# Hybrid trunk in Strassen pairs: value sums into SBUF, conv borders kept in the tile, gate weights split at another place, and more instructions tied to written order

## The chip, the cores and the metric

The kernel runs on one core of a Trainium2 chip. Five engines of the core have queues of their own and are synchronised by semaphores: TensorE (PE in the profile; its weight loads are PEld), VectorE (DVE), ScalarE (ACT), GpSimd (POOL) and SyncE (SP), which here only issues DMAs. Each queue is worked off in its order. The metric is the device time of one execution in microseconds; lower is better. The time of a kernel is the median of several executions; beside it stands one execution taken with the profiler, from which all rows of the profile come.

## The reference

Two layers of a decoder trunk on 1024 tokens of width 1024, all in float32. A layer normalises x, projects it with one wide matrix, runs four mLSTM heads and four retention heads of width 256 in chunks, gates them and projects back.

```python
for l in range(DEPTH):                                   # DEPTH = 2
    ada = silu(c) @ w_ada[l] + b_ada[l]
    shift, scale, gate = split(ada, 3)
    h = rmsnorm(x, norm_g[l]) * (1 + scale) + shift
    p = h @ w_in[l]
    mq, mk, mv, mo, mz, mi, mf, rq, rk, rv, rz = split_cols(p)
    qk = silu(causal_dwconv(concat(mq, mk), conv_w[l], conv_b[l]))   # 4 taps along the tokens
    cell = mlstm_chunkwise(*heads(qk), heads(mv), mi + b_igate[l], mf + b_fgate[l])
    y_m = sigmoid(mo) * head_layernorm(cell, gn_m[l]) * silu(mz)
    ret = retention_chunkwise(rotary(rq), rotary(rk), rv)
    y_r = head_layernorm(ret, gn_r[l]) * silu(rz)
    x = x + gate * (concat(y_m, y_r) @ w_out[l])
return rmsnorm(x, final_g)
```

causal_dwconv is a sum of four products of a weight with the input shifted by 0 to 3 tokens.

## The kernel before, in words

**Numbers in two parts.** Every operand of a matmul is kept as a high part (a copy rounded to the fp32r format, on ACT) and a low part (the difference, on POOL or DVE); mm3 (L172 to L175) makes three matmuls of a product: high·high, high·low, low·high. For a weight these are `high` (L397, the copy at L399) and `low` (L402, the subtraction at L404). For data it is `split_to` (L853: the copy at L854, the subtraction at L855).

**Strassen pairs.** Two column blocks of the projection and the two halves of the tokens make a 2 × 2 product, computed with seven block products, a11, a12, S1, S2, S3, S4, a22. `quad` (L682) prepares the weights. A plain weight is a load from SP; S1 and S3 are a load and then a second DMA, issued from POOL, that adds another block onto it (`add`, L693); S2 and S4 are sums on DVE (`total`, L697). The `Feeder` issues these steps by slot numbers: the load eight slots ahead of use, the add six, the high copy some four, the low part two. One slot is one product of twelve matmuls or two of them. The products are added up in three PSUM banks X, Y and Z: `pair_product` (L741) for q, k, z and o, `vpair_product` (L769) for the values. In the latter, a11 is copied out of X (L802) and added to what Y holds; before, the sum stood in Y itself (L803) and `store` read it from there in two steps, the high copy on ACT (L774) and the subtraction on DVE (L779).

**The order of the work.** PE's order is written out by hand for the whole kernel. `launch` puts a generator of follow-up work on a list; `tick`, called after each product, advances those whose time has come; the number after a `yield` is how many ticks later it goes on. On the other engines Tile's scheduler decides the order by its own estimate of times, within priorities, except for instructions that are marked with `late` (L133): those stay in the order in which the program was written, behind everything written earlier on that engine. `Later()` does the same for a string of DVE instructions. The start of layer 0 (from L1416, until startup.\_\_exit\_\_) is a script of two- to four-letter steps that fixes the order on all engines: Ann a step of the conditioning's sums, Tnn transposes of x, Hnn, Enn, Unn, Cnn the modulation (L1515, L1517, L1521, L1525), Fnn and fnn the first matmuls (L1473 to L1477), Pn and Gn the sums and the resulting scales, Wnn and wnn weights.

**Gate weights.** The input and forget gates have eight columns of weights. `gate_raw` (L474) loads them into a tile wgr, of which there is one buffer; `gate_units` (L480) spreads them into a 36-column tile in two parts (L485 fills the gap with zeros, then two `split_to`) and multiplies. `gate_chain` (L495) then computes the running gate sums on DVE with a helper whose instructions show as L140, and PE transposes them (L554, the tiles T4). `rotary_tables` is another long string of small DVE instructions of layer 0.

**Convolution.** `conv_chain` (L857) scales the last tap on ACT (L861), adds three shifted taps on DVE (L867), applies tanh (L872) and multiplies (L874). The first half of the tokens leaves its last three columns in a small tile, halo (L863); in the second half the taps cover only 511, 510 and 509 columns, and three tiny instructions (L869) add what comes over the border from the halo.

**Attention.** `attention` loads chunks of q and k back from DRAM, splits them (`split_qk`, L983: ACT's L854 and POOL's L855 with q and kc), and the scores multiply q with kc. Small statistics go over DVE and POOL (L1150 to L1164).

**Plan.** A string lists the order of the pair jobs in each layer: v45 are the values of heads 4 and 5, q4 and k4 the query and key of head 4, z4 its gate path, a10 a z and an o block together.

Of the kernel before, what the change touches and what calls it, by code (L numbers as in the profile page):

```python
# [87 lines left out]
def tile_hybrid_trunk(ctx, tc, x, xt, c, positions, w_ada, b_ada, norm_g, w_in, w_blk, w_val, conv_w, conv_b,  # L88
# [23 lines left out]
    def wt(tag, n, bufs, dt=F32):  # L112
        return wrk.tile([P, n], dt, tag=tag, bufs=bufs, name=nm(tag))

# [15 lines left out]
    def f(ap):  # L130
        return ap.bitcast(F32)

    def late(ins):  # L133
        tc.keep_in_program_order(ins)
        return ins
# [343 lines left out]

    def gate_units(gr, hT, pgs):  # L480
        wg = (wt("cH", 516, 1, F32R)[:, 0:KT * 36], wt("cL", 516, 1, F32R)[:, 0:KT * 36])
        gr3 = gr.rearrange("p (k g) -> p k g", k=KT)
        w3 = [w.rearrange("p (k g) -> p k g", k=KT) for w in wg]
        for w in w3:
            A.activation(w[:, :, 4:32], ones.unsqueeze(1).to_broadcast([P, KT, 28]), AF.Copy, scale=0.0)  # L485
        for a, b in ((0, 4), (32, 0)):
            split_to((w3[0][:, :, a:a + 4], w3[1][:, :, a:a + 4]), gr3[:, :, b:b + 4], V)
        for half in range(2):
            pg = ps_a()
            for k in range(KT):  # L490
                mm3(pg[0:36, :], [w[:, k * 36:(k + 1) * 36] for w in wg], hT[k][half], k == 0, k == KT - 1)
            pgs.append(pg)
            yield

    def gate_chain(l, pgs, gt):  # L495
# [19 lines left out]
        for half in range(2):  # L515
            A.activation(es[half][0:4], es[half][0:4], AF.Ln, bias=ones[0:4, 0:1])
        yield 7
        T4s = []
# [141 lines left out]
    class Feeder:  # L660
# [21 lines left out]
        def quad(self, blk, at, u):  # L682
            raw, r, h = {}, {}, {}
            a11, a12, a21, a22 = blk[0][0], blk[0][1], blk[1][0], blk[1][1]

            def ev(t, fn, *args):
                self.events.append((t, lambda: fn(*args)))

            def load(n, src):
                raw[n] = ring_load(src)  # L690

            def add(n, src):
                G.dma_start(raw[n], src, accum_op=ALU.add)  # L693

            def total(n, one, two):
                raw[n] = raw[one]
                V.tensor_tensor(raw[n], raw[one], raw[two], ALU.add)  # L697

            def hi(n):
                h[n] = high(raw[n])  # L700

            def lo(n, eng):
                r[n] = low(h[n], raw[n], eng)

            for n, one, two in (("S1", a21, a22), ("S3", a21, a11)):
                ev(at[n] - 8, load, n, one)
                ev(at[n] - 6, add, n, two)
            for n, src in (("a11", a11), ("a12", a12), ("a22", a22)):
                ev(at[n] - 7 + u, load, n, src)
            for n in at:  # L710
                if n not in ("S2", "S4"):
                    ev(at[n] - 4 + u, hi, n)
                    ev(at[n] - 2, lo, n, G if n in POOL_LOW else V)
            T2, T4 = at["S2"], at["S4"]
            ev(T2 - 4, total, "S2", "a11", "S1")
            if at["a12"] < T2:
                ev(T2 - 3, total, "S4", "a12", "S2")
            ev(T2 - 4 + u, hi, "S2")
            ev(T2 - 2 - (T4 - T2 < 3), lo, "S2", V)
            if at["a12"] > T2:  # L720
                ev(T4 - 3, total, "S4", "S2", "a12")
            ev(T4 - 4 + u, hi, "S4")
            ev(T4 - 2, lo, "S4", V)
            return r, h
# [15 lines left out]

    def pair_product(F, done, loose=False):  # L741
        bank, keep = {}, {}

        def product(n, part, w):
            b, form = PRODUCT[n]
            new = b not in bank
            if new:
                bank[b] = ps_x() if b == "X" else ps_z()
            for k in range(4):
                mm3(bank[b], w[k], F[form][k], new and k == 0, k == 3, b != "Y")  # L750
            with tc.high_priority():
                if n in ("a11", "S1", "S2"):
                    keep[n] = wt("acc", 512, NACC)
                    A.copy(keep[n], bank[b])  # L754
                elif n == "a12":
                    c = keep["a11"] if loose else bank["Y"]
                    V.tensor_tensor(c, bank["Y"], keep["a11"], ALU.add)
                    done(0, 0, c)
                elif n == "S3":
                    V.tensor_tensor(keep["S1"], bank["X"], keep["S1"], ALU.add)  # L760
                    done(1, 1, keep["S1"])
                elif n == "S4":
                    V.tensor_tensor(keep["S2"], bank["Z"], keep["S2"], ALU.add)  # L763
                    done(0, 1, keep["S2"])
                else:
                    done(1, 0, bank["X"])
        return product

    def vpair_product(l, F, heads):  # L769
# [15 lines left out]
        def product(n, part, w):  # L785
# [13 lines left out]
            with tc.high_priority():  # L799
                if n == "a11":  # L800
                    c = wt("acc", 512, NACC)
                    A.copy(c, bank["X"])  # L802
                    V.tensor_tensor(bank["Y"], bank["Y"], c, ALU.add)  # L803
                    launch(store(part, 0, 0, bank["Y"]))
                    del bank["Y"]
                elif n in ("S1", "S2"):
# [49 lines left out]

    def conv_chain(l, hg, which, m, half, pt, halo):  # L857
        cl = cols[l][0]
        ct = which * 8 + hg * 2 + m
        acc = wt("acc", 512, NACC)  # L860
        A.activation(acc, pt, AF.Identity, bias=cl[:, 8 + ct:9 + ct], scale=cl[:, 72 + ct:73 + ct])  # L861
        if half == 0:
            V.tensor_copy(halo, pt[:, HALF - 3:HALF])  # L863
        yield 1
        for d in range(1, 4):
            wcol = cl[:, 24 + 16 * (3 - d) + ct:25 + 16 * (3 - d) + ct]
            V.scalar_tensor_tensor(acc[:, d:], pt[:, 0:HALF - d], wcol, acc[:, d:], ALU.mult, ALU.add)  # L867
            if half:
                V.scalar_tensor_tensor(acc[:, 0:d], halo[:, 3 - d:3], wcol, acc[:, 0:d], ALU.mult, ALU.add)  # L869
        yield 1  # L870
# [46 lines left out]
    def conv_done(l, hg, which):  # L917
        halos = [wt("halo", 3, 4) for _ in range(2)]
        late = []

        def one(m, half, src, delay=0):
            launch(conv_chain(l, hg, which, m, half, src, halos[m]), delay)

        def done(m, half, src):
            if m and half:
                late.append(src)
                return
            one(m, half, src)
            if m:
                one(1, 1, late[0], 1)  # L930
        return done
# [34 lines left out]
    def attention(l, hg, gt):  # L966
# [16 lines left out]
        def split_qk(what, j):  # L983
            if j < NCH:
                raw = raws.pop((what, j))
                t = wt("q", 1024, 2, F32R) if what == "q" else wt("kc", 1024, 1, F32R)
                (kx if what == "k" else qs)[j] = t
                split_to((t[:, 0:512], t[:, 512:1024]), raw)

# [367 lines left out]
    def norm_later(l, xn, sq, hT, half, keep, gaps):  # L1357
# [19 lines left out]
        for k in range(KT):  # L1377
            gain, shift = gsh[l][:, 0, k:k + 1], gsh[l][:, 1, k:k + 1]
            hT[k][half] = (bt(F32R), bt(F32R))
            V.tensor_tensor(xn[k], xn[k], R, ALU.mult)  # L1380
            A.activation(hT[k][half][0], xn[k], AF.Identity, scale=gain, bias=shift)
# [73 lines left out]
    for l in range(DEPTH):  # L1455
# [23 lines left out]
        if l == 0:  # L1479
# [10 lines left out]
            for step in script.split():  # L1490
# [46 lines left out]
                elif what == "P":  # L1537
                    ada_sums(0, arg[0], accs[arg[0]], pad)
                elif what == "G":
                    n = arg[0]  # L1540
# [9 lines left out]
            head_cols(0, hrows)  # L1550
            startup.__exit__(None, None, None)
        else:
            for half in range(2):
                for k in range(KT):
                    first(half, k)
                    tick()
                if half == 0:
                    drain()
        for half in range(2):
            z_evac(gp, 0)(half, pf[0][half])  # L1560
            o_evac(gp, 0, gdr[l][0])(half, pf[1][half])
            z_evac(gp, 1)(half, pf[2][half])
        if l == 0:
            for r in ring3:
                A.activation(r[:, :, HD:HD + 2], ident[:, 0:8].rearrange("p (a c) -> p a c", a=4), AF.Copy, scale=0.0)
                A.copy(r[:, 0:2, HD:HD + 1], rmask[:, 254:256].unsqueeze(2))
        F = {}
        launch(build_forms(hT, F))
        run_units(gate_units(gate_raw(l) if l else vgr, hT, pgs))
        launch(gate_chain(l, pgs, gt), 1)  # L1570
        if l == 0:
# [7 lines left out]
        plan = ("v45 v67 z4 q4 k4 z5 q5 k5 v01 q6 k6 q7 z6 k7 q0 a10 k0 v23 q1 k1 a11 q2 k2 q3 a20 k3 z7 a21 a30 a31",  # L1579
                "v45 q4 k4 z4 q5 k5 v67 q6 k6 z5 q7 k7 v01 q0 k0 z6 a10 q1 k1 v23 q2 k2 a11 q3 k3 a20 z7 a21 a30 a31")[l]  # L1580
        jobs = [(w[0], [int(d) for d in w[1:]]) for w in plan.split()]
# [17 lines left out]
        def job_product(what, arg):  # L1599
# [10 lines left out]
            if h > 3:  # L1610
                return pair_product(F, rot_done(l, h, which, *rot), True)
            return pair_product(F, conv_done(l, h, which))

# [86 lines left out]
```

## Time and profile before

| | us |
|---|---|
| median of three executions (lowest, highest) | 2282.63 (2281.71, 2287.09) |
| the profiled execution | 2286.23 |
| its span, first to last instruction | 2284.5 |
| mean granted clock of TensorE in it, as a share of full speed | 0.972 |

How to read the rows: L174 is line 174 of the kernel. An entry such as "PE pz L173 <- DVE acc L779: 16.0, 3, 7.6" means that PE's instructions of L173 which write a tile pz stood still for 16.0 us in all, three times, at most 7.6, until DVE's instruction of L779 had written acc. In a row of the timeline the first number is the start, the second the duration, and the bracket the idle time of that engine before it and what ended it. A row of windows gives the stretch, its length, the busy time of PE, PEld, DVE, ACT and POOL with the number of instructions, then the granted clock of TensorE, the share of the DMA engines and the rate in GB/s. A group's row gives count, then busy us in all and mean ns, then idle time of the engine before it and what ended it.

### The profile page before, as it was taken

To read this page: it belongs to the slowest core of one execution; us is meant where nothing else is said; L and a number is where in the kernel's file an instruction comes from. 1 tells how busy PE (TensorE), PEld (TensorE's weight loads), DVE (VectorE), ACT (ScalarE), POOL (GpSimd) and SP (SyncE) were. 2 spreads that over 40 slices of the span, in tenths; PEclk is the share of its full clock that TensorE was granted. 3 is DMA by queue.
4 is the path that set the end of the run, shared out by engine and by line. 5 is a ranking of instruction groups with operands and counts; after the bars stand their busy time and mean duration, and the time that the engine had idled before them with its cause. 6 is when DMAs were issued, how large, how long until landed. Compare 5 with 4: busy or idle time off the path is not lost. (4 is left out here: it accounts for less than half of the span.)

```text
span 2284.5 us, 35248 instructions
## 1 busy us (share of the span) xinstructions
PE 2134.0 (93%) x11483; PEld 1840.7 (81%) x11483; DVE 1827.6 (80%) x3301; ACT 1150.6 (50%) x2157; POOL 957.2 (42%) x842
## 2 busy tenths in 40 slices
PE   5979899999999998999999799999999899899998
PEld 3778789878897877888787788988988888688887
DVE  5898888888979999893627989698697789977653
ACT  5634344444555656653456333544555555565442
POOL 0343244444354544514266434544635353442323
PEclk8999999999999999999999899999999999999999
DMA  8247678887686767686633676877867677576974
GB/s 261 66 116 217 192 233 228 237 240 190 180 244 166 191 183 188 194 268 212 215 126 79 201 197 194 245 193 204 245 159 207 183 205 196 155 205 198 261 256 118
DMA packets 452549, 448.32 MB, mean 196 GB/s; under 512 B 191218, under 2 KB 309754, under 8 KB 452364
## 3 DMA queue, kind: packets, MB, share of 16 engines
q1 hardware_dynamic: 432636, 410.14, 58.0%
q0 software_dynamic: 19584, 35.66, 10.4%
q8 instruction: 90, 1.47, 0.3%
q14 instruction: 95, 0.78, 0.1%
q10 hardware_dynamic: 144, 0.26, 0.0%
HBM read 322.69 MB, written 123.24 MB: 195 GB/s over the span
## 5 line engine op out<-in xcount | busy, mean ns | idle before, releaser
L399 ACT CAST wH<-R 128x512 fp32r<-128x512 f32 x616 | 378.2, 618 | 463.7 <-PE px L174 122.1
L404 POOL TENSOR_TENSOR R<-R,wH 128x512 fp32r<-128x512 f32 x276 | 395.9, 1441 | 508.1 <-ACT wH L399 344.2
L173 PE MATMUL px<-b,wH 128*128 128x512 f32 x912 | 365.1, 400 | 11.1 <-ACT acc L754 8.2
L174 PE MATMUL px<-b,wH 128*128 128x512 f32 x912 | 362.7, 398 | 0.0
L175 PE MATMUL px<-b,R 128*128 128x512 f32 x912 | 361.7, 397 | 0.0
L404 DVE TENSOR_TENSOR R<-R,wH 128x512 fp32r<-128x512 f32 x340 | 258.4, 764 | 112.3 <-ACT wH L399 107.5
L174 PE MATMUL pz<-b,wH 128*128 128x512 f32 x704 | 276.2, 392 | 5.1 <-DVE b L1251 5.1
L173 PE MATMUL pz<-b,wH 128*128 128x512 f32 x704 | 276.6, 393 | 1.9 <-DVE acc L763 1.8
L175 PE MATMUL pz<-b,R 128*128 128x512 f32 x704 | 275.3, 391 | 0.0
L173 PEld LDWEIGHTS px<-b,wH 128*128 128x128 f32 x912 | 176.0, 193 | 49.3 <-ACT acc L754 10.2
L175 PEld LDWEIGHTS px<-b,R 128*128 128x128 f32 x912 | 175.6, 193 | 38.4
L174 PEld LDWEIGHTS px<-b,wH 128*128 128x128 f32 x912 | 175.9, 193 | 34.1
L173 PE MATMUL px<-wH,b 128*128 128x256 f32 (+1 forms) x576 | 176.3, 306 | 18.3 <-DVE acc L867 6.3
L693 POOL DMA_DIRECT2D R<-in_w_blk_dram x104 | 92.4, 889 | 207.7 <-DMA R<-in_w_blk_dram 90.6
L174 PE MATMUL px<-R,b 128*128 128x256 f32 (+1 forms) x576 | 174.6, 303 | 4.2 <-DVE R L404 4.2
L175 PE MATMUL px<-wH,b 128*128 128x256 f32 (+1 forms) x576 | 174.2, 302 | 0.0
L174 PEld LDWEIGHTS pz<-b,wH 128*128 128x128 f32 x704 | 132.9, 189 | 31.4 <-DVE b L1251 6.4
L175 PEld LDWEIGHTS pz<-b,R 128*128 128x128 f32 x704 | 132.9, 189 | 28.4
L173 PEld LDWEIGHTS pz<-b,wH 128*128 128x128 f32 x704 | 132.9, 189 | 28.3 <-DVE acc L763 2.2
L173 PE MATMUL pz<-wH,b 128*128 128x256 f32 (+1 forms) x448 | 135.8, 303 | 17.3 <-DVE acc L779 16.0
L175 PE MATMUL pz<-wH,b 128*128 128x256 f32 (+1 forms) x448 | 135.2, 302 | 0.7 <-DVE b L1251 0.7
L174 PE MATMUL pz<-R,b 128*128 128x256 f32 (+1 forms) x448 | 135.1, 302 | 0.0
(359 smaller groups left out, 5346.7 us busy)
## 6 DMA issues: line engine op xcount, KB each, us to landing
R<-in_w_blk_dram SPq DMA_DIRECT2D x276, 256.0 KB
vdr<-acc SPq DMA_DIRECT2D x128, 256.0 KB
ring<-vdr SPq DMA_DIRECT2D x64, 512.0 KB
R<-in_w_out_dram SPq DMA_DIRECT2D x128, 256.0 KB
R<-in_w_blk_dram POOLq DMA_DIRECT2D x104, 256.0 KB, 4.5
R<-in_w_val_dram SPq DMA_DIRECT2D x80, 256.0 KB
gdr<-acc SPq DMA_DIRECT2D x64, 256.0 KB
acc<-in_w_ada_dram SPq DMA_DIRECT2D x64, 256.0 KB
```

The source lines that it names most:

```text
L173: PE.matmul(o, lt[0], rt[0], start=start, stop=False, skip_group_check=more)
L174: PE.matmul(o, lt[0], rt[1], start=False, stop=False, skip_group_check=more)
L175: PE.matmul(o, lt[1], rt[0], start=False, stop=stop, skip_group_check=more)
L399: A.copy(h, r)
L404: eng.tensor_tensor(lo, r, f(h), ALU.subtract)
L693: G.dma_start(raw[n], src, accum_op=ALU.add)
```

## The change

1. The gate weights' split is a function of its own, `gate_weights`, tied to written order. In layer 0 it is a step X of the startup script, after f04; in layer 1 the load is issued before the first matmuls and the split stands after the first half of them.
2. `gate_chain` pauses 12 ticks instead of 7 before its sums.
3. In `vpair_product` the sum of a11 goes into the SBUF tile c; the bank Y isn't written any more.
4. Accumulator tiles are 516 wide. `pair_product` keeps S1 and S2 at column 3 of a tile of 515, and the last three columns of the other half's result are copied in front of them. A second-half convolution then reads 512 columns at three shifts, and the L869 instructions are gone.
5. `late` marks nothing while layer 0's startup is recorded. From there on these are tied as well: the accumulating DMAs, DVE's weight sums, the q and k splits, the filling of constant columns of the ring tiles, and the multiplication of the first half's normalisation at the layer's end.
6. In layer 1's plan z4 stands ahead of q4 and k4.

```diff
     def wt(tag, n, bufs, dt=F32):
-        return wrk.tile([P, n], dt, tag=tag, bufs=bufs, name=nm(tag))
+        t = wrk.tile([P, 516 if tag == "acc" else n], dt, tag=tag, bufs=bufs, name=nm(tag))
+        return t[:, 0:n] if tag == "acc" else t
...
+    planned = [False]
+
     def late(ins):
-        tc.keep_in_program_order(ins)
+        if planned[0]:
+            tc.keep_in_program_order(ins)
         return ins
...
-    def gate_units(gr, hT, pgs):
+    def gate_weights(gr):
         wg = (wt("cH", 516, 1, F32R)[:, 0:KT * 36], wt("cL", 516, 1, F32R)[:, 0:KT * 36])
...
-            A.activation(w[:, :, 4:32], ones.unsqueeze(1).to_broadcast([P, KT, 28]), AF.Copy, scale=0.0)
+            late(A.activation(w[:, :, 4:32], ones.unsqueeze(1).to_broadcast([P, KT, 28]), AF.Copy, scale=0.0))
         for a, b in ((0, 4), (32, 0)):
-            split_to((w3[0][:, :, a:a + 4], w3[1][:, :, a:a + 4]), gr3[:, :, b:b + 4], V)
+            late(A.copy(w3[0][:, :, a:a + 4], gr3[:, :, b:b + 4]))
+            late(V.tensor_tensor(w3[1][:, :, a:a + 4], gr3[:, :, b:b + 4], f(w3[0][:, :, a:a + 4]), ALU.subtract))
+        return wg
+
+    def gate_units(wg, hT, pgs):
...
-        yield 7
+        yield 12
...
             def add(n, src):
-                G.dma_start(raw[n], src, accum_op=ALU.add)
+                late(G.dma_start(raw[n], src, accum_op=ALU.add))
...
-                V.tensor_tensor(raw[n], raw[one], raw[two], ALU.add)
+                late(V.tensor_tensor(raw[n], raw[one], raw[two], ALU.add))
...
-    def pair_product(F, done, loose=False):
-        bank, keep = {}, {}
+    def pair_product(F, done, loose=False, conv=False):
+        bank, keep, full = {}, {}, {}
+
+        def halo(n, pt):
+            if conv:
+                V.tensor_copy(full[n][:, 0:3], pt[:, HALF - 3:HALF])
...
                 if n in ("a11", "S1", "S2"):
-                    keep[n] = wt("acc", 512, NACC)
+                    full[n] = wt("acc", 515, NACC)
+                    keep[n] = full[n][:, 3:515]
                     A.copy(keep[n], bank[b])
                 elif n == "a12":
...
                     V.tensor_tensor(c, bank["Y"], keep["a11"], ALU.add)
+                    halo("S2", c)
                     done(0, 0, c)
...
-                    done(1, 1, keep["S1"])
+                    done(1, 1, full["S1"] if conv else keep["S1"])
...
-                    done(0, 1, keep["S2"])
+                    done(0, 1, full["S2"] if conv else keep["S2"])
                 else:
+                    halo("S1", bank["X"])
                     done(1, 0, bank["X"])
...
-                    V.tensor_tensor(bank["Y"], bank["Y"], c, ALU.add)
-                    launch(store(part, 0, 0, bank["Y"]))
-                    del bank["Y"]
+                    V.tensor_tensor(c, bank["Y"], c, ALU.add)
+                    launch(store(part, 0, 0, c))
...
-        A.activation(acc, pt, AF.Identity, bias=cl[:, 8 + ct:9 + ct], scale=cl[:, 72 + ct:73 + ct])
-        if half == 0:
-            V.tensor_copy(halo, pt[:, HALF - 3:HALF])
+        o = 3 * half
+        A.activation(acc, pt[:, o:o + HALF], AF.Identity, bias=cl[:, 8 + ct:9 + ct], scale=cl[:, 72 + ct:73 + ct])
...
-            V.scalar_tensor_tensor(acc[:, d:], pt[:, 0:HALF - d], wcol, acc[:, d:], ALU.mult, ALU.add)
-            if half:
-                V.scalar_tensor_tensor(acc[:, 0:d], halo[:, 3 - d:3], wcol, acc[:, 0:d], ALU.mult, ALU.add)
+            e = 0 if half else d
+            V.scalar_tensor_tensor(acc[:, e:], pt[:, o + e - d:o + HALF - d], wcol, acc[:, e:], ALU.mult, ALU.add)
...
-                split_to((t[:, 0:512], t[:, 512:1024]), raw)
+                late(A.copy(t[:, 0:512], raw))
+                late(G.tensor_tensor(t[:, 512:1024], raw, f(t[:, 0:512]), ALU.subtract))
...
-            V.tensor_tensor(xn[k], xn[k], R, ALU.mult)
+            (V if half else Later()).tensor_tensor(xn[k], xn[k], R, ALU.mult)
...
-                      "H14 f04 U05 E14 T17 F05 A35 H15 U14 E15 A36 f05 C17 U15 F14 A37 f14 P3 F15 G3 H06 E06 "
+                      "H14 f04 X U05 E14 T17 F05 A35 H15 U14 E15 A36 f05 C17 U15 F14 A37 f14 P3 F15 G3 H06 E06 "
...
+                elif what == "X":
+                    wg = gate_weights(vgr)
...
             startup.__exit__(None, None, None)
+            planned[0] = True
         else:
+            gr = gate_raw(l)
             for half in range(2):
...
                 if half == 0:
                     drain()
+                    wg = gate_weights(gr)
...
-                A.activation(r[:, :, HD:HD + 2], ident[:, 0:8].rearrange("p (a c) -> p a c", a=4), AF.Copy, scale=0.0)
-                A.copy(r[:, 0:2, HD:HD + 1], rmask[:, 254:256].unsqueeze(2))
+                late(A.activation(r[:, :, HD:HD + 2], ident[:, 0:8].rearrange("p (a c) -> p a c", a=4), AF.Copy,
+                                  scale=0.0))
+                late(A.copy(r[:, 0:2, HD:HD + 1], rmask[:, 254:256].unsqueeze(2)))
...
-        run_units(gate_units(gate_raw(l) if l else vgr, hT, pgs))
+        run_units(gate_units(wg, hT, pgs))
...
-                "v45 q4 k4 z4 q5 k5 v67 q6 k6 z5 q7 k7 v01 q0 k0 z6 a10 q1 k1 v23 q2 k2 a11 q3 k3 a20 z7 a21 a30 a31")[l]
+                "v45 z4 q4 k4 q5 k5 v67 q6 k6 z5 q7 k7 v01 q0 k0 z6 a10 q1 k1 v23 q2 k2 a11 q3 k3 a20 z7 a21 a30 a31")[l]
```

More of the change, by code (lines that the diff above doesn't have):

```diff
@@ L855, in split_to, with conv_chain @@
         eng.tensor_tensor(dst[1], src, f(dst[0]), ALU.subtract)
-    def conv_chain(l, hg, which, m, half, pt, halo):
+    def conv_chain(l, hg, which, m, half, pt):
         cl = cols[l][0]
@@ L917, in conv_done @@
     def conv_done(l, hg, which):
-        halos = [wt("halo", 3, 4) for _ in range(2)]
-        late = []
+        late_one = []
         def one(m, half, src, delay=0):
-            launch(conv_chain(l, hg, which, m, half, src, halos[m]), delay)
+            launch(conv_chain(l, hg, which, m, half, src), delay)
         def done(m, half, src):
             if m and half:
-                late.append(src)
+                late_one.append(src)
                 return
@@ L929, in done @@
             if m:
-                one(1, 1, late[0], 1)
+                one(1, 1, late_one[0], 1)
         return done
@@ L1611, in job_product @@
                 return pair_product(F, rot_done(l, h, which, *rot), True)
-            return pair_product(F, conv_done(l, h, which))
+            return pair_product(F, conv_done(l, h, which), conv=True)
         going, forms, left = {}, {}, {}
```

## The prediction

> **What bounds the kernel now.** I read the page first, then the list of waits, then the granted clock around the long ones.
>
> ```profile
> span 2284.5 us, 35248 instructions
> PE 2134.0 (93%) x11483; PEld 1840.7 (81%) x11483; DVE 1827.6 (80%) x3301; ACT 1150.6 (50%) x2157; POOL 957.2 (42%) x842
> ```
>
> TensorE (PE) bounds it: it is idle for 2284.5 − 2134.0 = 150.5 us, and the change leaves its matmuls and nearly all their order alone. So a gain can only come out of those 150.5 us and out of a low clock behind them. PE's list of waits says who ends them (releaser, total, times, longest):
>
> ```profile
> PE pz L173 <- DVE acc L779: 16.0, 3, 7.6
> PE pa L175 <- DVE b L909: 15.3, 7, 5.3
> PE pz L1473 <- ACT b L1515: 12.9, 1, 12.9
> PE px L173 <- DVE acc L867: 7.8, 4, 5.5
> ```
>
> The windows (PE, PEld, DVE, ACT, POOL busy, then the granted clock) show a second price. The first one holds a wait of 2.65 us and stays at full clock. The others begin as PE resumes, each after a wait of 4 us or more.
>
> ```profile
> 126.00:134.00 8.00, 3.33 (x26) 2.95 (x25) 8.00 (x9) 2.78 (x6) 6.12 (x4) 1.00 0.09 33
> 46.40:52.40 6.00, 5.93 (x20) 4.96 (x20) 2.92 (x5) 4.19 (x8) 0.00 (x0) 0.52 0.41 98
> 139.40:144.60 5.20, 5.05 (x24) 5.08 (x25) 5.14 (x10) 1.24 (x2) 1.41 (x2) 0.52 0.62 176
> 176.90:181.10 4.20, 4.15 (x20) 4.15 (x21) 4.18 (x14) 0.59 (x1) 0.00 (x0) 0.50 0.96 216
> 245.40:250.20 4.80, 4.78 (x11) 3.80 (x12) 3.54 (x6) 1.18 (x2) 0.00 (x0) 0.50 0.92 281
> 1267.10:1271.00 3.90, 3.85 (x19) 3.88 (x20) 3.90 (x4) 0.00 (x0) 3.48 (x3) 0.53 0.65 202
> 1285.00:1290.80 5.80, 5.75 (x27) 5.78 (x28) 5.69 (x11) 1.45 (x3) 0.88 (x1) 0.50 0.73 200
> 1800.60:1806.40 5.80, 5.73 (x27) 5.73 (x28) 5.56 (x16) 2.96 (x6) 3.12 (x5) 0.50 0.33 82
> 1997.10:2000.90 3.80, 3.78 (x11) 3.20 (x12) 3.80 (x9) 1.09 (x2) 0.55 (x1) 0.50 0.36 134
> ```
>
> A long wait costs its length and then (1 − clock) × the stretch: 6.0 × 0.48 = 2.9 us at 46, 5.2 × 0.48 = 2.5 at 139, 4.2 × 0.50 = 2.1 at 177, 2.4 at 245, 1.8 at 1267, 2.9 at 1285, 2.9 at 1800, 1.9 at 1997. A removed wait gives both back; a new one pays both.
>
> **The change part by part.** The durations are those of the profiled execution, which took 2286.23 us (1.73 around its span).
>
> *Gate weights to step X.* ACT's timeline, PE's one row and SP's one:
>
> ```profile
> 45.40 0.34 ACT L854 CAST cH<-wgr 128x32 fp32r<-128x32 f32 x2 [13.89 <-DMA wgr<-in_w_in_dram]
> 45.65 0.77 ACT L1515 ACTIVATE b<-pa,gsh 128x512 fp32r<-128x512 f32 x1
> 63.34 0.59 ACT L1511 COPY b<-pa 128x512 f32<-128x512 f32 x1 [2.81 <-PE pa L378]
> 46.47 0.80 PE L1473 MATMUL pz<-b,wH 128*128 128x512 f32 x1 [12.90 <-ACT b L1515]
> 47.09 1.04 SPq L394 DMA_DIRECT2D R<-in_w_blk_dram  x2
> ```
>
> The small copy at 45.40 stands ahead of L1515 on ACT and waits 13.89 us for a load; the evacuation that PE needs queues behind it. In the new order the copies come after step f04, where before had about 68 us. ACT then goes from 31.5 to the next transposes (32.2) and to L1515, about 33.1 with its 0.77; PE resumes near 33.5, where its work before ended. Gain: 12.5 of the 12.90, plus 2.9 of clock. What is late next: a weight load of 47.09 whose copy ACT now reaches near 46.6, some 3 us early; ACT's idle 2.81 at 63.34, which moves up as well, hides all but about 0.4. If it did not, 3 us more are lost. The copies at X take about 1 us of ACT, inside similar gaps. On SP only layer 1's small gate load moves, from ahead of that weight load to six loads behind it. I take −15, bounds −11 and −15.4.
>
> *Value sums into SBUF, and the gate chain's yield of 12 instead of 7* (layer 0's first stage):
>
> ```profile
> 120.00:180.00 60.00, 44.34 (x330) 43.24 (x331) 59.55 (x92) 18.42 (x32) 23.36 (x15) 0.87 0.50 134
> 120.67 0.69 DVE L803 TENSOR_TENSOR pz<-pz,acc 128x512 f32<-128x512 f32 x1
> 128.04 0.68 DVE L779 TENSOR_TENSOR acc<-pz,acc 128x512 fp32r<-128x512 f32 x1
> PE px L173 <- ACT acc L754: 5.6, 2, 5.2
> PE pa L554 <- DVE cL L140: 4.0, 1, 4.0
> PE pz L173 <- DVE acc L763: 1.8, 1, 1.8
> ```
>
> L803 left its sum in the bank, so PE's next product waited until L779 had read it, 128.04 + 0.68. Now the bank is free at 120.67 + 0.69, and the waits on L779 go. But DVE is busy 59.55 of 60 us while PE is idle for 15.7: its backlog stays. Running down DVE's queue in the new order with the durations of the old timeline, PE is owed 8.4 us up to the gate transposes (L554) instead of about 15.5, since much of the gate chain now stands behind what PE needs. That is −7.4. The waits on the bank copy L754 (5.6) and on L763 (1.8) turn into one of about 3.9 on a weights' sum, now tied behind some 25 rotary-table instructions: −3.5. The three clock stretches are worth 7.0; short waits remain, so I take half. Together −14.4, bounds 0 (all returned by the backlog) and −23.
>
> *The same in layer 1, and z4 ahead of q4, k4:*
>
> ```profile
> PE pz L173 <- DVE acc L779: 5.8, 1, 5.8
> PE px L173 <- DVE acc L810: 4.6, 1, 4.6
> PE px L173 <- ACT acc L754: 2.6, 1, 2.6
> PE px L174 <- DVE R L404: 2.0, 1, 2.0
> ```
>
> 15.0 us of waits. In the new order I count 2.6 left of them, and a new one of 4 where L341 now needs a split (DVE, ACT, POOL in a row) only one matmul after its source: −8.4, and half of the clock's 1.8 + 2.9. I take −10.7, bounds −3 and −18.
>
> *q and k splits tied to written order.* POOL's q and k subtractions now stand behind whatever was written before them. At two scores (q against kc, PE's second row) that is a small POOL op fed by DVE's L763, which needs the matmul of PE's first row, ending at 849.28:
>
> ```profile
> 848.88 0.40 PE L175 MATMUL pz<-b,R 128*128 128x512 f32 x1
> 849.24 0.28 PE L174 MATMUL pa<-q,kc 128*128 128x256 f32 x1
> 853.98 0.67 DVE L763 TENSOR_TENSOR acc<-pz,acc 128x512 f32<-128x512 f32 x1
> 853.91 0.14 DVE L1159 TENSOR_TENSOR va<-va,mv 128x2 f32<-128x2 f32 x1
> 854.13 0.71 POOL L1160 TENSOR_TENSOR rsd<-va,mhalf 128x2 f32<-128x2 f32 x1 [2.88 <-DVE va L1159]
> 856.01 1.29 POOL L855 TENSOR_TENSOR kc<-acc,kc 128x512 fp32r<-128x512 f32 x1 [1.16 <-issue]
> ```
>
> 0.67 + 0.14 + 0.71 + 2 × 1.29 = 4.1 us of new wait; before, the splits were 47 matmuls ahead. A like chain stands before the scores at 574.9 (estimate from the same durations plus one weights' low part: 3.2). With 1.8 of clock for each: +11. Everywhere else the splits keep 23 matmuls or more. Bounds 0 (DVE and POOL early) and +17 (each queue 3 us late).
>
> *Borders and second-half convolutions.*
>
> ```profile
> L869 DVE SCALAR_TENSOR_TENSOR acc<-halo,cols,acc 128x1 f32<-128x1 f32 (+2 forms) x96 | 37.2, 388 | 0.0
> ```
>
> These 96 go, 37.2 us of DVE, most under PE's matmuls; the halo copies stay. They lie in front of L867's and L909's followers, and the order gives the longest waits of both (5.5 at 1800, 5.3 at 1997) 63 and 24 matmuls more room. With clock 10.8 + 4.8 = 15.6, of which I take two thirds; of the other 12.3 of the two rows a quarter. −13, bounds 0 and −28.
>
> *Weights' adds, sums and ring fills tied; four more ACT table loads.*
>
> ```profile
> L693 POOL DMA_DIRECT2D R<-in_w_blk_dram x104 | 92.4, 889 | 207.7 <-DMA R<-in_w_blk_dram 90.6
> 98.20 1.28 ACT L511 ACT_TABLE_LOAD   x1
> 99.50 0.63 ACT L511 ACTIVATE dm<-dm 4x512 f32<-4x512 f32 x1
> ```
>
> The adds come a median of 46 matmuls later on POOL, where their load has landed more often (90.6 us of POOL's idle time were for that), and the hi copy still follows 71 matmuls behind. Behind a waiting add stand the splits, priced above. Table loads: 4 × 1.28 = 5.1 us of ACT, which is 50% busy. I take +2, bounds 0 and +5.1.
>
> The Trainium skill speaks against this part: "ScalarE: Activation LUTs", What ACT_TABLE_LOAD costs, has a drain of about 1380 ns beside the 1283 ns of a load, 2.66 us in all. By it the upper bound would be 10.6 us (an estimate from that page). The trace disagrees: the next activation starts 0.02 us after the load's end.
>
> *Reshuffle.* About 930 of 3155 DVE instructions, 554 of ACT's and 258 of POOL's stand elsewhere, some ten places off. I price what I can't list at a wait or two like L554's 4.0: +6, bounds −10 and +20.
>
> **Sum.** −15 − 14.4 − 10.7 + 11 − 13 + 2 + 6 = −34.1, so 2252.1 for the profiled execution. That execution lay 3.6 above the median of the runs (2282.63): 2248.5, told as 2248.
>
> The Trainium skill, "TensorE: Matmul & The Clock Gate", Part 1, has one idle window of about 3.4 us for the fall to half clock and one busy window for the return, so 1.7 us for each long wait. By that estimate the clock's shares above shrink and the sum is about 2250. The rows give 1.8 to 2.9, so they decide.
>
> **The rivals.**
> 1. *VectorE's backlog takes the first stages back.* For it: 59.55 of 60 us busy. Then the two first stages give −4 and −3 in place of −25.1: 2248 + 18 = 2266. Against: the gate chain does move behind.
> 2. *The attention's waits go whole.* Borders −28, the first stages −22 and −17, no new reshuffle cost and no clock paid at the splits: 2248 − 15 − 13.9 − 6 − 3.6 = 2210. Against: L909 waits on chains that the change doesn't shorten.
> 3. *Slower: POOL in written order.* 128 splits now stand behind other POOL work; if one in four comes 2 us late, 32 × 2 = 64 replace the 11: 2248 + 53 = 2301. It decides from 46 us, 23 of 128 late by 2. For it: POOL is one queue with 207.7 us of idle time at adds alone. Against: 23 matmuls are some 5 us, the chain about 4.
> 4. *The estimate-ordered engines undo it:* the stall at 46 goes, and reshuffled queues cost as much elsewhere, 2282.
>
> **How the numbers follow.** Forecast 0.50 (own range 2236 to 2260), rival 1 0.19, rival 2 0.12, rival 3 0.11, rival 4 0.08. What this kernel's runs can tell from no change is 0.3%, 6.8 us. Faster: 0.50 + 0.19 + 0.12 and 0.02 of rival 4, 0.83; same 0.05; slower 0.11 and 0.01, 0.12. The range runs from 2218, cutting half of rival 2, to 2279, cutting rival 3 and half of rival 4.
>
> **What would show it.** Right: no ACT wait on wgr and PE's 12.90 gone; no PE wait on the value path's subtraction; shorter waits near 140 and 1267, with fewer half-clock stretches; waits of 3 to 5 us at the two scores, ended by POOL. Wrong: many PE waits on POOL's q and k splits (rival 3); PE idle 15 us between 120 and 180 still (rival 1); a new wait of several us in the first 60 us would undo the first term.

## The result and the profile after

The changed kernel is slower: 2303.01 us median of five executions (2293.66 to 2307.11) against 2281.71 of before, ratio 1.0086, 95% interval 1.0063 to 1.0109. Forecast was 2248, range 2218 to 2279. The profiled execution took 2305.66. The page of the changed kernel begins:

```profile
span 2303.9 us, 35078 instructions
PE 2164.8 (94%) x11483; PEld 1839.9 (80%) x11483; DVE 1823.7 (79%) x3205; ACT 1154.7 (50%) x2161; POOL 962.8 (42%) x842
```

TensorE's idle time did fall, from 150.5 to 2303.9 − 2164.8 = 139.1 us. But its busy time rose by 30.8 us with the same 11483 matmuls, at the same mean granted clock of 0.972. I had not looked for a loss there. One window in layer 0's output projection, in which PE is busy without a break at full clock, shows it; the first row is of before, the second of the changed kernel (length, then PE busy with its matmuls, PEld, DVE, ACT, POOL, clock):

```profile
1130.00:1180.00 50.00, 50.00 (x223) 41.39 (x222) 6.18 (x9) 26.31 (x41) 38.25 (x31) 1.00 0.48 152
```

```profile
1130.00:1180.00 50.00, 50.00 (x216) 40.27 (x215) 19.65 (x19) 26.16 (x41) 40.70 (x30) 1.00 0.48 151
```

In the same 50 us, 223 matmuls became 216, 3% fewer. Over the whole trace the starts of successive 512-column matmuls at full clock lie about 227 ns apart before (mean over some 6100 of them, pauses left out) and about 232 after; those of 256 columns kept their 119 to 120 ns.

PE's waits in the changed kernel (releaser, total, times, longest):

```profile
PE px L177 <- ACT acc L817: 32.3, 8, 8.0
PE pa L178 <- POOL q L1000: 16.5, 10, 4.5
PE pa L179 <- DVE b L921: 14.4, 6, 3.8
PE px L177 <- DVE acc L824: 8.6, 2, 4.9
...
PE pa L179 <- POOL kc L1000: 6.6, 9, 1.3
...
PE pa L562 <- DVE cL L144: 3.5, 1, 3.5
...
PE px L177 <- ACT acc L767: 2.6, 1, 2.6
```

Lines are those of the changed kernel: L817 was L802, L1000 was L855, L921 was L909, L824 was L810, L767 was L754, L562 was L554. The wait of 12.90 on L1515 is gone, and so are the 16.0 on the value subtraction. In their place stand 32.3 us on L817, the copy of bank X for the value sum (before: 5.6), and the scores' waits on q and kc, 23.1 in these two rows. The first long wait on L817 in the timelines of POOL, DVE, ACT and PE in turn (start, duration, and in the bracket the idle time before):

```profile
103.20 2.99 POOL L869 TENSOR_TENSOR b<-acc,b 128x512 fp32r<-128x512 f32 x2
106.13 2.80 POOL L701 DMA_DIRECT2D R<-in_w_val_dram  x3
```

```profile
110.39 0.69 DVE L705 TENSOR_TENSOR R<-R,R 128x512 f32<-128x512 f32 x1 [6.61 <-DMA R<-in_w_val_dram]
```

```profile
111.11 0.62 ACT L403 CAST wH<-R 128x512 fp32r<-128x512 f32 x1 [8.18 <-DVE R L705]
113.35 1.14 ACT L403 CAST wH<-R 128x512 fp32r<-128x512 f32 x2 [1.62 <-DVE R L705]
114.39 0.58 ACT L817 COPY acc<-px 128x512 f32<-128x512 f32 x1
```

```profile
115.02 0.58 PE L177 MATMUL px<-wH,b 128*128 128x256 f32 x1 [7.73 <-ACT acc L817]
```

L817 is not slow (0.58). It queues on ACT behind three high copies, these wait for DVE's weight sums L705, and the first of those stood 6.61 us until an accumulating DMA had landed. POOL issued that DMA only at 106.13, when it was through with two splits of data (L869) that stand ahead of it. Read from the end, the row of PE names ACT; only the bracket of DVE names the add.

### The profile page after: what moved, and what is told of

Read it like the earlier page. It is cut to its first block, busy times and chain, and to the rows that moved or that the text cites. A ratio compares the mean times of both kernels' runs of the same rounds, so it can differ in the third digit from the quotient of the medians.

```text
span 2303.9 us, 35078 instructions
## 1 busy us (share of the span) xinstructions
PE 2164.8 (94%) x11483; PEld 1839.9 (80%) x11483; DVE 1823.7 (79%) x3205; ACT 1154.7 (50%) x2161; POOL 962.8 (42%) x842
## 5 line engine op out<-in xcount | busy, mean ns | idle before, releaser
L403 ACT CAST wH<-R 128x512 fp32r<-128x512 f32 x616 | 372.8, 618 | 565.5 <-DVE R L705 118.7
L179 PE MATMUL px<-b,R 128*128 128x512 f32 x912 | 366.5, 402 | 1.1 <-DVE R L408 1.1
L178 PE MATMUL pz<-b,wH 128*128 128x512 f32 x704 | 280.2, 398 | 1.1 <-DVE b L1263 1.1
L179 PE MATMUL pz<-b,R 128*128 128x512 f32 x704 | 280.6, 399 | 0.0
L177 PE MATMUL pz<-b,wH 128*128 128x512 f32 x704 | 280.2, 398 | 0.0
L177 PE MATMUL px<-wH,b 128*128 128x256 f32 (+1 forms) x576 | 179.2, 311 | 43.4 <-ACT acc L817 32.3
L179 PE MATMUL px<-wH,b 128*128 128x256 f32 (+1 forms) x576 | 177.0, 307 | 0.0
L177 PEld LDWEIGHTS px<-wH,b 128*128 128x128 f32 x576 | 116.9, 203 | 48.3 <-ACT acc L817 34.0
L1000 POOL TENSOR_TENSOR kc<-acc,kc 128x512 fp32r<-128x512 f32 x64 | 94.2, 1471 | 133.3 <-ACT kc L999 123.0
```

The costliest lines, as they stand in the source:

```text
L177: PE.matmul(o, lt[0], rt[0], start=start, stop=False, skip_group_check=more)
L178: PE.matmul(o, lt[0], rt[1], start=False, stop=False, skip_group_check=more)
L179: PE.matmul(o, lt[1], rt[0], start=False, stop=stop, skip_group_check=more)
L403: A.copy(h, r)
L1000: late(G.tensor_tensor(t[:, 512:1024], raw, f(t[:, 0:512]), ALU.subtract))
```

## The experiments

Ratios are to the kernel before, run on the same chip; 1% is 22.8 us. Where I compare two kernels I subtract ratios.

**e1 and e5, e10, e16: what slowed the matmuls.** First the width of the accumulators alone.

```diff
-        return wrk.tile([P, n], dt, tag=tag, bufs=bufs, name=nm(tag))
+        t = wrk.tile([P, 516 if tag == "acc" else n], dt, tag=tag, bufs=bufs, name=nm(tag))
+        return t[:, 0:n] if tag == "acc" else t
```

> The kernel before with one thing of the change: accumulator tiles 516 columns wide, of which 512 are used, so that the tiles behind them in SBUF (the weights' high parts wH among them) lie 384 bytes further on. In the changed kernel successive matmuls of 512 columns start 233 ns apart in place of 227 at full clock, from the startup on, and TensorE's busy time is 30.8 us longer with the same matmuls. Theory A, the tiles' addresses do it: spacing 232 to 234 here too, PE busy about 2165, time 25 to 37 us above the kernel before. Rival B, it is a matter of the chip or of the single execution: spacing near 227, time within 5 us of before (and if the spacing is 233 with the time unchanged, B as well). Rival C, the order of the other engines' work does it: spacing near 227, time within 7 us.

Measured: 1.0053 (1.0035 to 1.0070), 2289.64 us, with 232 ns between the matmuls. Theory A holds in the spacing, B and C fall: e2, run on the same chip, kept 227. Its times were too high: the cost is 12 us and not 25 to 37, and PE was busy for 2148.2 us and not 2165. In the profiled execution, the fastest of the ten, PE's idle time fell to 2279.4 − 2148.2 = 131.2 and the mean granted clock rose to 0.979, so a good part of the slowdown came back as shorter waits and less half clock. Then a pad in place of wider accumulators; e10 has 64 columns and e16 has 32 where e5 has 96:

```diff
+        if tag == "acc" and not padded:
+            padded.append(wrk.tile([P, 96], F32, tag="pad", bufs=1, name=nm("pad")))
+            V.memset(padded[0], 0.0)
```

> The kernel before with an unused tile of 384 bytes between the accumulator tiles and the weights' high parts wH (and one small memset for it): accumulators as before, everything behind them 384 bytes further on, as in the changed kernel. Theory A1, where the later tiles lie (wH above all, which the matmuls load as weights) slows the matmuls: spacing 232 to 234 ns, 10 to 20 us above the kernel before, like e1. Rival A2, the accumulators' own stride of 2080 bytes does it: spacing 227, time within 6 us of before.

> The kernel before with an unused tile of 256 bytes (e5 had 384) ahead of wH. A3 in the form modulo 256: spacing 227, time within 6 us of the kernel before. A3 in the form modulo 512, and A4: spacing above 230, 10 to 20 us slower like e5.

> The kernel before with an unused tile of 128 bytes ahead of wH. Modulo-256 theory: spacing of 512-column matmuls 231 to 234 ns, as with 384. If 227, 384 was special for another reason.

The same window as above, of e5 (384 bytes), e10 (256) and e16 (128) in turn:

```profile
1130.00:1180.00 50.00, 50.00 (x216) 40.26 (x215) 6.56 (x10) 25.98 (x40) 37.66 (x30) 1.00 0.45 149
```

```profile
1130.00:1180.00 50.00, 50.00 (x223) 41.39 (x222) 7.14 (x11) 26.62 (x42) 37.92 (x30) 1.00 0.51 157
```

```profile
1130.00:1180.00 50.00, 50.00 (x216) 40.26 (x215) 5.43 (x8) 25.95 (x40) 37.52 (x31) 1.00 0.47 147
```

e5: 1.0052 (1.0031 to 1.0073), 232 ns. e10: 1.0012 (0.9996 to 1.0029), 227 ns. e16: one execution, 2296.61 us, 232 ns. So it is not the accumulators' stride but where the tiles behind them lie: with a move by 128 or 384 bytes the matmuls are slower, with one by 256 they are not. In the compiled programs the weights' tiles R and wH and the data tiles b of the kernel before all start at the same address modulo 256 (64); after the change the high parts wH start at 192. Which of the moved tiles matters was not tried one by one; of the moved ones, the matmuls in that window read only wH, there as the moving operand of 512 columns.

**e2: the gate weights alone.**

```diff
-                      "H14 f04 U05 E14 T17 F05 A35 H15 U14 E15 A36 f05 C17 U15 F14 A37 f14 P3 F15 G3 H06 E06 "
+                      "H14 f04 X U05 E14 T17 F05 A35 H15 U14 E15 A36 f05 C17 U15 F14 A37 f14 P3 F15 G3 H06 E06 "
...
+                elif what == "X":
+                    wg = gate_weights(vgr)
```

> The kernel before with the gate weights' split of layer 0 at step X of the startup and nothing else of the change (layer 1 as before). My first term: PE's wait of 12.90 us and the half clock behind it go, 13 to 15 us faster (2267 to 2269). Rival: the gain is lost again in layer 0's first stage, where PE then runs into weights that are not there yet: less than 6 us faster. Matmul spacing 227 ns under theories A and C; under B it may be 233, and then the changed kernel's spacing says nothing.

Measured: 0.9964 (0.9947 to 0.9980), 2268.54 us: 8 us (5 to 12), between what the expectation and its rival gave. In its profile the 100th matmul starts 14.6 us earlier than before, as forecast; by the 300th it is 11.3. What is late next, PE and then ACT:

```profile
42.91 0.50 PE L1480 MATMUL pz<-b,wH 128*128 128x512 f32 x1 [1.27 <-DVE b L1528]
```

```profile
50.33 0.62 ACT L399 CAST wH<-R 128x512 fp32r<-128x512 f32 x1 [3.35 <-DMA R<-in_w_blk_dram]
```

The second is the weight load that I had named. The first follows a 1.90 us wait of DVE at 41.11 for a conditioning load that I had taken to be in time.

**e3, e4, e11, e12, e6: the ties.** Each takes late( ) away from some of these lines of the changed kernel: e3 the first, e12 the second, e11 both, e4 the third and fourth, e6 all.

```diff
-                late(G.dma_start(raw[n], src, accum_op=ALU.add))
+                G.dma_start(raw[n], src, accum_op=ALU.add)
...
-                late(V.tensor_tensor(raw[n], raw[one], raw[two], ALU.add))
+                V.tensor_tensor(raw[n], raw[one], raw[two], ALU.add)
...
-                late(A.copy(t[:, 0:512], raw))
-                late(G.tensor_tensor(t[:, 512:1024], raw, f(t[:, 0:512]), ALU.subtract))
+                split_to((t[:, 0:512], t[:, 512:1024]), raw)
```

> The changed kernel with the accumulating DMAs not tied. Theory D: the ties make the adds late, DVE's sums and ACT's high copies wait for their landing, and the bank copies L817 queue behind those copies (32.3 us of PE's waits in 8 places). Untied, these fall to below 10 us and the time by 15 to 25 us. Rival E: the value path itself makes L817 late (its accumulator is held longer since the sum stays in it): waits of 25 to 35 us remain, time within 7 us of the changed kernel's 2303.

> The changed kernel with the q and k splits not tied. Theory F: the waits of the scores on POOL's and ACT's q and kc (16.5 + 6.6 + 2.0 + 1.4 = 26.5 us) go, and with half clock behind some of them the time falls by 15 to 28 us. Rival: the scores' waits come back in other places of the attention (before: 8.0 on L1059, 7.6 on L1116), so that less than 8 us is won.

> The changed kernel with adds and DVE's weight sums untied, the q and k splits still tied. e3 (adds free) had 2288, e6 (all free) 2263. Theory D2, the sums are the other 25 us (DVE stands in order behind a load or a backlog): 2262 to 2272. Rival F2, the splits are, and only show when the adds are free: 2282 to 2292, with some 25 us of waits of the scores on q and kc.

> The changed kernel with only DVE's weight sums untied. D2: below 2292, more than 10 us off the changed kernel, waits on L817 nearly as before since the adds still land late. F2, or the adds alone set when a sum can start: within 6 us of 2303.

> The changed kernel without three kinds of ties: the adds, DVE's weight sums, and the q and k splits are left to the scheduler. e3 (adds alone) took off 15 us, e4 (splits alone) nothing. Theory D+: adds and sums are one chain and the splits cost nothing net: 2278 to 2288, waits on L817 below 13 us. Rival G, each tie covers for another and without all of them the gain of the first stage shows: 2262 to 2275. Spacing stays near 233 in both.

| still tied | kernel | ratio (95%) | us |
|---|---|---|---|
| adds, sums, splits | changed | 1.0086 (1.0063 to 1.0109) | 2303.01 |
| sums, splits | e3 | 1.0042 (1.0017 to 1.0066) | 2288.04 |
| adds, splits | e12 | 1.0109 (1.0087 to 1.0132) | 2309.07 |
| splits | e11 | 1.0049 (1.0031 to 1.0066) | 2293.68 |
| adds, sums | e4 | 1.0128 (1.0097 to 1.0160) | 2304.70 |
| none of these | e6 | 0.9924 (0.9899 to 0.9949) | 2263.01 |

The three ties together cost 1.62%, 37 us. They don't add up: adds and sums tied alone cost 2.04%, 46 us (e4 against e6), splits alone 1.25%, 28 us (e11 against e6). Freeing one of them in the changed kernel therefore shows little: nothing for the splits (theory F's waits went, others came), nothing for the sums, 10 us for the adds. e6 fell in the range of its rival G, but not for the reason given there: e13 below finds no gain of the first stage. e11 lies closest to F2. Waits of e4, then of e11, then of e6:

```profile
PE px L177 <- ACT acc L817: 27.5, 7, 8.6
```

```profile
PE pa L178 <- POOL q L1000: 14.1, 9, 3.4
...
PE px L177 <- ACT acc L817: 5.3, 4, 1.8
...
PE pa L179 <- POOL kc L1000: 4.6, 5, 1.3
```

```profile
PE px L177 <- DVE acc L824: 12.3, 2, 7.4
PE pa L1114 <- POOL sL L1071: 9.4, 7, 2.7
PE px L177 <- ACT acc L817: 9.4, 5, 3.0
```

With adds and sums tied the waits are on L817, with the splits tied on q and kc: two different losses. Which of the pair it is, the same row of e3 (adds free) and of e12 (sums free) tells:

```profile
PE px L177 <- ACT acc L817: 12.6, 6, 4.3
```

```profile
PE px L177 <- ACT acc L817: 27.3, 6, 8.3
```

Wherever the adds are tied, L817 costs 27 to 32 us of waits, wherever they are free 5 to 13. And freeing the sums gains nothing, whether the adds are tied (e12 against the changed kernel) or free (e11 against e3), so D2 falls. So of that pair it is the adds. Both comparisons have the splits tied; with the splits free, adds and sums were not run apart.

**e7 and e8: the borders.** e7 is e6 with borders and accumulators as before (the diff of the border part taken back), e8 is the changed kernel with the same, ties kept.

> The changed kernel without those ties and with borders and accumulators as before: gate weights, yield, value sums in SBUF and plan are what is left of the change. Accumulators of 512 put wH back to its old address: spacing 227 under A1 and A2. By my terms 2 and 3 this gains 15 + 14 + 11 = 40 us; e2 measured 9 of the 15. Theory H, the first stage gives what I priced: 2245 to 2256. Rival 1 of the prediction, VectorE's backlog takes it back: 2262 to 2270, no better than e2 (2268.5).

> The changed kernel, all ties kept, with borders and accumulators as before (512 wide, halo tiles, the L869 instructions). Theory A: spacing 227, and the time falls by 8 to 20 us below the changed kernel's 2303. Rival, the borders' 37 us of DVE work are worth more than the slower matmuls cost: spacing 227 but 2303 or above.

e7: 0.9976 (0.9957 to 0.9996), 2275.81 us, 227 ns: theory H falls, and the kernel is even slower than rival 1's 2262 to 2270. e8: 1.0093 (1.0058 to 1.0128), 2304.07 us, 227 ns. Under the ties the faster matmuls of e8 were worth no more than the borders it gave up, so its rival came out. What the borders are worth by themselves needs e9.

**e9: a version that beats both.** e6 with 32 columns of pad behind the accumulators, so that wH lies 512 bytes from its old place.

```diff
+        if tag == "acc" and not padded:
+            padded.append(wrk.tile([P, 32], F32, tag="pad", bufs=1, name=nm("pad")))
+            V.memset(padded[0], 0.0)
```

> The kernel of e6 (no ties of adds, sums, splits; 2263) with an unused tile of 128 bytes behind the accumulators, so that wH lies 512 bytes from its place before in place of 384. Theory A3, what counts is an address of wH modulo 512 (or 256) that equals the one before: spacing back at 227 ns, 10 to 16 us below e6, 2247 to 2253, faster than both kernels by over 1%. Rival A4, any move from the old place costs: spacing 232 to 233, time 2258 to 2267.

0.9871 (0.9851 to 0.9890), 2254.44 us, 227 ns: 12 us below e6, as A3 had it, and 1.3% faster than before. Against e7 it differs by the borders (and the pad): 1.05%, 24 us.

**e13, e14, e15: why the first stage gives nothing.** From e9, e14 takes layer 1's old plan, e15 the yield of 7, e13 both and the value sum in the bank:

```diff
-                    V.tensor_tensor(c, bank["Y"], c, ALU.add)
-                    launch(store(part, 0, 0, c))
+                    V.tensor_tensor(bank["Y"], bank["Y"], c, ALU.add)
+                    launch(store(part, 0, 0, bank["Y"]))
+                    del bank["Y"]
```

> The kernel of e9 (2254.4, no ties, wH moved by 512 bytes) without the first-stage part: value sums in the bank as before, yield 7, plan as before; gate weights and borders as in the change. Theory I, the first stage wins 9 us at the bank and gives it back at the bank copy L772 and at the gate transposes: within 5 us of e9, 2249 to 2259, with the waits on the value subtraction (14 to 16 us) back and those on the transposes and L350 shorter. Theory J, the part is a loss, since e7 was 7 us slower than e2: 2242 to 2249, the fastest of all. Theory H, it is worth what I priced: 2265 or more.

> The kernel of e9 with layer 1's old plan (q4 k4 ahead of z4). Theory I: layer 1's waits at the transposes and L350 (3.1 + 4.6 in e9) shrink, 3 to 8 us faster. Rival: they stay, since the gate chain's later start causes them, and the time is within 4 us of e9.

> The kernel of e9 with the gate chain's pause back at 7. Theory K, the later chain pushes its work onto what PE needs next (L772 in layer 0, L350 in layer 1): those waits shrink by 3 us or more each, 4 to 10 us faster. Rival: the chain's work comes back ahead of the value sums, waits near 134 and 1246 grow, 0 to 8 us slower.

e13: 0.9845 (0.9822 to 0.9869), 2249.91 us, the fastest of all; e14: 0.9884 (0.9854 to 0.9914), 2256.37; e15: 0.9880 (0.9851 to 0.9911), 2256.52. The intervals of e13 and e9 overlap: the part is worth nothing (theory I), or costs some 6 us (J); theory H falls again. Plan and yield alone change nothing, as the rivals of e14 and e15 had it. PE's long waits there, first of e13, then of e9:

```profile
128.62 0.55 PE L182 MATMUL pz<-wH,b 128*128 128x256 f32 x1 [7.58 <-DVE acc L799]
```

```profile
134.10 0.58 PE L182 MATMUL px<-wH,b 128*128 128x256 f32 x1 [7.39 <-DVE acc L829]
...
230.12 0.79 PE L182 MATMUL px<-b,wH 128*128 128x512 f32 x1 [6.07 <-ACT acc L772]
...
1286.96 1.12 PE L567 MATMUL pa<-ident,cL 128*128 128x128 f32 x4 [3.08 <-DVE cL L149]
...
1292.66 0.80 PE L350 MATMUL pa<-wH,ones_r 128*128 128x512 f32 x1 [4.58 <-ACT wH L873]
```

The wait on the value subtraction (L799 in e13) turns into one on L829, another DVE instruction of the value path, of the same length a few products later; and e9 waits 6.07 at the bank copy of 230, where e2 waited 2.75 and e13 2.15. By the starts of the same matmul, e9 is 9.2 us ahead of e13 at the 800th and 1.7 at the 1200th; in layer 1 it is 11.7 ahead at the 6300th and 2.4 at the 6600th. In both layers the gain is made and then given back within a few hundred matmuls.

## Why the prediction was wrong, point by point

**The failed step is the price of the tied adds and sums.** The prediction said: "The adds come a median of 46 matmuls later on POOL, where their load has landed more often", and "the hi copy still follows 71 matmuls behind": +2, bounds 0 and +5.1. The first half was right and misled. These rows are of the changed kernel; of before the prediction shows L693's 207.7, and the rows of L697 and L399 are here in front:

```profile
L697 DVE TENSOR_TENSOR R<-R,R 128x512 f32<-128x512 f32 x136 | 108.3, 797 | 0.8
L399 ACT CAST wH<-R 128x512 fp32r<-128x512 f32 x616 | 378.2, 618 | 463.7 <-PE px L174 122.1 <-PE pz L174 55.5 <-issue 41.0
```

```profile
L701 POOL DMA_DIRECT2D R<-in_w_blk_dram x104 | 91.4, 884 | 81.2 <-PE px L179 29.5 <-DMA R<-in_w_blk_dram 22.2 <-DVE acc L144 8.5
L705 DVE TENSOR_TENSOR R<-R,R 128x512 f32<-128x512 f32 x136 | 110.6, 818 | 25.3 <-DMA R<-in_w_val_dram 18.0 <-issue 5.3 <-DMA R<-in_w_blk_dram 2.0
L403 ACT CAST wH<-R 128x512 fp32r<-128x512 f32 x616 | 372.8, 618 | 565.5 <-DVE R L705 118.7 <-PE px L178 79.9 <-DMA R<-in_w_blk_dram 76.4
```

POOL's idle time at the adds fell from 207.7 to 81.2 us, as I had said. The waiting moved to the other end of the transfer: DVE's sums went from 0.8 us of idle time to 25.3, and ACT's copies now wait 118.7 us for sums (before: 40.4) and 76.4 for landings, which are not among the three largest entries before. What stands behind a waiting copy on ACT is a bank copy, and behind that PE. The largest entry is not the one that counts. What ended ACT's idle time before these copies in e3 (adds free), then in e12 (sums free), in us and times:

```profile
  DVE R L705: 105.6, 54
  DMA R<-in_w_blk_dram: 23.5, 9
```

```profile
  DMA R<-in_w_blk_dram: 75.5, 29
  DVE R L705: 47.1, 18
```

The wait for landings falls with the adds' tie. The wait for sums falls with the sums' tie, and that gains nothing. I counted matmuls between the add and its reader and took them for time in hand. But POOL's place in that count is its place in the queue, not the time at which it gets there. Measured for adds and sums together: 46 us where the splits are free (e4 against e6), 10 to 14 for the adds where they are tied (changed against e3, e12 against e11), in place of +2 with an upper bound of 5.1.

**The splits** were the right fear at the wrong size. At the two scores I named, PE waits a little longer than worked out, 4.5 us and 1.3 at 851 (4.1 forecast), 2.8 and 1.3 at 576 (3.2 forecast):

```profile
850.92 0.39 PE L178 MATMUL pa<-q,kc 128*128 128x256 f32 x1 [4.52 <-POOL q L1000]
852.60 0.58 PE L179 MATMUL pa<-q,kc 128*128 128x256 f32 x1 [1.29 <-POOL kc L1000]
```

But "Everywhere else the splits keep 23 matmuls or more" did not protect the rest: by the list of waits the scores wait 19 times, and the tie costs 28 us (e11 against e6), against my +11 and its bound of +17. Rival 3 gave the outcome, 2301 with a chance of 0.11, by a mechanism of this kind; but its place was the q and k splits alone, at 64 us where they cost 28, and it left the other gains standing. That its number is so near is luck.

**A term that was missing.** The wider accumulators move wH by 384 bytes: 12 us (e1, e5, and e6 against e9). The prediction has no term for part 4's tile width: it said that the change leaves PE's matmuls alone and looked for gains and losses in PE's idle time only, and its bounds for the unlisted were set by reordered queues.

**Gate weights:** right in mechanism, −15 forecast, −8 measured (5 to 12), short of my bound of 11, which the interval still reaches. In the profile the start is 14.6 us earlier at the 100th matmul and 11.3 at the 300th, because loads behind the removed wait are late in turn.

**First stage of both layers**, the second step that failed: −25.1 forecast, nothing or a loss measured (e9 against e13). Here rival 1 was right: DVE's backlog takes the freed bank back. The bank's wait did go, and up to the 800th matmul the gain was there, 9.2 us. But the sum I ran down DVE's queue stopped at the gate transposes, and what it left behind came due at 230 and near 1290.

**Borders:** −13 forecast with a bound of −28; 24 measured once ties and addresses are out of the way. Mis-sized, in the other direction.

**The sum, redone**, along a chain of kernels from before to the changed one: −8 (gate weights of layer 0, e2 against before) + 3 (first stage, e7 against e2) − 24 (borders, e9 against e7) + 12 (addresses, e6 against e9) + 37 (ties, changed against e6) = +20; measured 0.86%, 19.6. Each step starts where the one before it ended, so the sum has to come out: it splits the result up and is no check of it. The +3 also holds layer 1's gate weights, the ring fills' and normalisation's ties and the freed startup, none of which was run alone, and the reshuffle, +6 in the forecast, is somewhere in these steps. Against the forecast of −34.1 the first stages are 28 us short and the ties 24 dearer (37 for 11 + 2); the addresses add 12 and the gate weights 7, while the borders came out 11 better and the reshuffle's 6 is not seen apart.

## What to carry to other kernels

Tying an instruction to written order fixes its place, not its time: before counting distance in another engine's work, ask what the queue does until it gets there, and look for the wait on the reader's side of the transfer. Compare the start-to-start spacing of the bound engine's instructions before and after, not its idle time alone: a tile made a few columns wider can shift every address behind it. And ties that together cost a lot can seem to cost nothing when they are freed singly, so free all suspected ties at once before freeing them one by one.

## What was not expected of the hardware

Successive 512-column matmuls start about 227 ns apart or 232, by the place of the tiles behind the accumulators: moved by 0 (before), 256 (e10) or 512 bytes (e9) 227, by 128 (e16) or 384 bytes (e1, e5) 232. Matmuls of 256 columns don't show it (119 to 120 ns in both). The slowdown is 2% of each such matmul, some 6100 × 5 ns = 30 us in all, but the time grew by 12 us (e1, e5), 0.5%. Why the address matters, no run here shows.
